# A two-layer encoder on one core: the copy that ends each DMA transpose is queued twelve products behind its issue instead of eight, with three tiles for each of its buffers

## The chip, the cores and the metric

The kernel runs on one NeuronCore of a Trainium2 chip. The metric is the device time of one execution in microseconds (us). The core's engines run side by side, each through its own list of instructions in order: TensorE (PE) multiplies, VectorE (DVE) and ScalarE (ACT) work elementwise, GpSimd (POOL) does some small work, SyncE (SP) issues the DMAs. An instruction that waits holds up everything behind it on its own engine.

## The reference

The input is x with 256 tokens of 1024 float32 values. Two layers follow, then a last RMSNorm:

```python
for layer in range(2):
    h = rms_norm(x, ffn1_norm[layer])
    x = x + 0.5 * swiglu(h, ffn1_w_gate[layer], ffn1_w_up[layer], ffn1_w_down[layer])
    h = rms_norm(x, mix_norm[layer])
    x = x + (even_mixer(h, ...) if layer % 2 == 0 else odd_mixer(h, ...))
    h = rms_norm(x, ffn2_norm[layer])
    x = x + 0.5 * swiglu(h, ffn2_w_gate[layer], ffn2_w_up[layer], ffn2_w_down[layer])
return rms_norm(x, final_norm)

def swiglu(h, w_gate, w_up, w_down):
    return (silu(h @ w_gate) * (h @ w_up)) @ w_down    # 1024 -> 2816 -> 1024
```

The mixers are attention layers; the change does not touch them.

## The kernel before

**Stages.** There are six stages: feed-forward (0), even mixer (1), feed-forward (2), feed-forward (3), odd mixer (4), feed-forward (5). The tokens are two tiles of 128 (tt = 0 and 1). In the trace, stage 0 is about 0 to 205 us, stage 2 about 300 to 525, stage 3 about 525 to 700, stage 5 about 830 to the end.

**Products.** Every float32 weight piece is split into a high part (`hi`, ACT, line 474) and the rest (`lo`, DVE, line 477). A *product* is one call of `mm`: three matmuls (lines 466, 467, 468) of hi x high, lo x high, hi x low, each 128x128 by 128x512. The weights arrive in tiles `raw` through SP's queue (line 376); a `raw` tile is loaded anew once the last `lo` has been made of it.

**A feed-forward stage.** The 2816 hidden values are five chunks of 512 (numbered 0 to 4) and one of 256. In a plain chunk, 16 products make the gates of both token tiles and 16 the ups; for the 256 both lie in one weight piece and 16 products do. One or two chunks of each stage (chunk 2 in stages 0 and 5, chunks 1 and 3 in stages 2 and 3) are done by Strassen's scheme, seven products for eight (`seven_gates`). For those DVE also adds up weight blocks (`two<-raw`, `raw<-two,raw`, line 392) and ACT and DVE split the sums (`shi`, `slo`). Then the *down* part multiplies the gated values by w_down, also partly by sevens, which need sums of gated blocks (`quarters`, `k10h` and the like).

**The turn-over.** The gated values of one chunk and one token tile (`glu`, 128x512) have to be transposed before the down part can use them. [...] After it ACT makes the high part `g_h` (and parts of `quarters`), DVE the rest `g_l`. There are 48 turn-overs: 6 chunks x 2 token tiles x 4 stages.

**What sets the order.** The order of instructions on each engine is that of the Python code; nothing reorders it. Work beside the products is written as generators. `mm` calls `tick` after each product, and each `yield n` means "go on n ticks, that is n products, later". So `TURN_WAIT = [2, 8]` says: issue the DMA 2 products after the first copy, and queue the second copy 8 products after that. The delay is a place in the program, not a time: ACT gets to that place when all ACT work ahead of it is done, and there waits for the DMA. Weight splits are queued by a rate per tick. Tiles `glu` and `turned` come from rings (`bufs`) of 2.

Of the kernel before, what the change touches and what calls it, by code (L numbers as in the profile page):

```python
# [18 lines left out]
P = 128  # L19
# [33 lines left out]
X_WAIT = 5  # L53
R_WAIT = 3
GLU_WAIT = 6
TURN_WAIT = [2, 8]
NAT_WAIT = 2
ROPE_WAIT = [3, 3]
KB_WAIT = {
# [143 lines left out]
class Trunk:  # L203
# [342 lines left out]

    def turned_over(self, m, w):

        two = self.t([P, 512], "turned", 2)
        planes, back = (t.bitcast(U16)[:, : 2 * w] for t in (two, m))  # L550
        self.nc.scalar.copy(planes.rearrange("p (h c) -> p h c", h=2), back.rearrange("p (c h) -> p h c", h=2))  # L551
        yield TURN_WAIT[0]
        self.nc.sync.dma_start_transpose(back.rearrange("p (j t) -> p j t", t=P), planes)
        yield TURN_WAIT[1]
        self.nc.scalar.copy(planes.rearrange("p (c h) -> p h c", h=2), back.rearrange("p (h c) -> p h c", h=2))  # L555
        yield 1
        return two
# [96 lines left out]
    def ffn(self):  # L654
# [13 lines left out]

        def glu(tt, f0, w, u, s):
            yield 1  # L670
            m = self.t([P, 512], "glu", 2)
            nc.vector.scalar_tensor_tensor(m[:, :w], u[:, :w], self.now.r[tt], s[:, :w], op0=ALU.mult, op1=ALU.mult)  # L672
            self.spawn(transposed(tt, f0, w, m), GLU_WAIT)

        def transposed(tt, f0, w, m):
            n = w // P
            tb = yield from self.turned_over(m, w)
            pairs = [f for f in range(f0, f0 + n) if f in paired and f + 1 < f0 + n]
            parts = []
            for f in pairs:  # L680
                yield from quarters(tt, f, tb, f - f0)

            if tt == 1 and f0 + n - 2 in pairs:
                n -= 1
            yield from self.split_psum(tb, n, f"g{tt}_{f0}_", parts)
            for j, part in enumerate(parts):
                gT[tt][f0 + j] = part
            for f in pairs if tt == 1 else []:
                yield from sums_of(f)
# [61 lines left out]
        def seven_gates(f0, w, pairs7):  # L751

            while len(K) < 4:
                self.tick(False)
            self.rate = SEVEN_RATE[self.now.n]
            h, M, c = self.now.hT, {}, {}
            op = nc.vector.tensor_tensor

            def copy():
                yield 1  # L760
                c["m"] = self.t([P, 512], "glu", 2)
                nc.scalar.activation(c["m"], M["1"], AF.Copy)

            def common():

                yield 1
                while "m" not in c:
                    yield 1
                w = self.t([P, 512], "silu", 2)
                op(w, M["6"], c["m"], op=ALU.add)  # L770
                yield 1
                y = self.t([P, 512], "glu", 2)
                op(y, M["5"], w, op=ALU.subtract)
                yield 1
                nc.vector.scalar_tensor_tensor(w, M["7"], -1.0, w, op0=ALU.mult, op1=ALU.add)
                c["y"], c["w"] = y, w

            def first_gate():
                yield 1
                while "m" not in c:  # L780
                    yield 1
                s = self.t([P, 512], "silu", 2)
                op(s, M["00"], c["m"], op=ALU.add)
                yield 1
                nc.scalar.activation(s, s, AF.Silu, scale=self.now.r[0])
                c["s"] = s

            def up(tt, o, u, s):
                nc.vector.scalar_tensor_tensor(o, u, self.now.r[tt], s, op0=ALU.mult, op1=ALU.mult)
                self.spawn(transposed(tt, f0, w, o), GLU_WAIT)  # L790
                yield 1

            def rest():
                yield 1
                while "s" not in c or "w" not in c:
                    yield 1
                y, z, m = c["y"], c["w"], c["m"]
                op(y, M["01"], y, op=ALU.add)
                yield 1
                tasks.append(self.start(up(0, y, y, c["s"])))  # L800
                yield 1
                op(m, M["10"], z, op=ALU.add)
                yield 1
                nc.scalar.activation(m, m, AF.Silu, scale=self.now.r[1])
                op(z, M["5"], z, op=ALU.subtract)
                yield 1
                if "11" in M:
                    op(z, M["11"], z, op=ALU.add)
                    yield 1
                tasks.append(self.start(up(1, m, z, m)))  # L810

            def product(name, lh, piece, first, last):
                self.mm(M[name], lh, piece, first, last)

            n7 = KD // 2 - pairs7
            M.update((name, self.bank(tag)) for name, tag in [("00", "s"), ("01", "s"), ("10", "s")])
            if n7:
                M["11"] = self.bank("o")
            for q in range(KD // 2):
                k, first, last = 2 * q, q == n7, q == KD // 2 - 1  # L820
                if q < n7:
                    pieces = self.take(4)
                    for i in range(2):
                        for n, piece in enumerate(pieces[2 * i : 2 * i + 2]):
                            for tt in range(NT):
                                product(f"{tt}{n}", h[tt][k + i], piece, k + i == 0, tt == n == 1 and i == 1 and q + 1 == n7)
                    continue
                b11, b21, b22, t7, t5, t8, t6 = self.take(7)
                if first:
                    for task in tasks:  # L830
                        self.finish(task)
                    M.update((name, self.bank(tag)) for name, tag in [("1", "pj"), ("5", "pj"), ("7", "tp")])
                    M["6"] = self.bank("tp" if n7 else "o")
                j = q - (KD // 2 - most)
                product("1", h[0][k + 1], b11, first, last)
                if last:
                    self.start(copy())
                product("00", h[0][k], b21, q == 0, last)
                if last:
                    tasks.append(self.start(first_gate()))  # L840
                product("01", K[0][j], b22, q == 0, last)
                product("7", K[3][j], t7, first, last)
                product("5", K[2][j], t5, first, last)
                product("10", h[1][k], t8, q == 0, last)
                product("6", K[1][j], t6, first, last)
            self.start(common())
            tasks.append(self.start(rest()))

# [24 lines left out]
        w, V = FF_MIXED, self.take(KD)  # L873
# [52 lines left out]
        def combine():  # L926

            op = nc.vector.scalar_tensor_tensor
            x = lambda tt, i: self.x[tt][:, i * 512 : i * 512 + 512]
            more = lambda o, y: nc.vector.tensor_tensor(o, o, y, op=ALU.add)  # L930
            yield 1
            c = self.t([P, 512], "silu", 2)
            nc.scalar.activation(c, M["1"], AF.Copy, scale=0.5)
            op(x(0, 0), M["1"], 0.5, x(0, 0), op0=ALU.mult, op1=ALU.add)
            yield 1
            v = self.t([P, 512], "silu", 2)
            op(v, M["6"], 0.5, c, op0=ALU.mult, op1=ALU.add)
            yield 1
            w = self.t([P, 512], "glu", 2)
            op(w, M["7"], -0.5, v, op0=ALU.mult, op1=ALU.add)  # L940
            yield 1
            y = self.t([P, 512], "silu", 2)
            op(y, M["5"], 0.5, v, op0=ALU.mult, op1=ALU.subtract)
            yield 1
            more(x(0, 1), y)
            z = self.t([P, 512], "glu", 2)
            yield 1
            op(z, M["5"], 0.5, w, op0=ALU.mult, op1=ALU.subtract)
            yield 1
            more(x(1, 0), w)  # L950
            yield 1
            more(x(1, 1), z)
# [436 lines left out]
    def after(self, tt, sl, nxt):  # L1389
# [10 lines left out]
        h, w = sl.start // 512, sl.stop - sl.start  # L1400
        half = slice(512 * h, 512 * h + 512)
        x, gain = self.x[tt], self.last_gain
        sq = self.t([P, 512], "sq")
        v = self.two.tile([P, 1], F32, tag="last_v", name=self.name("v"), bufs=6)
        if (tt, h) in ((0, 1), (1, 0)):
            nc.scalar.activation(sq, x[:, sl], AF.Square, scale=D ** -0.5, accum_out=v)
# [8 lines left out]
        elif not h:  # L1415
            a, b = self.last_v[0]
# [146 lines left out]
```

## Time and profile before

| | before |
|---|---|
| median of 3 runs | 1030.58 us (1029.57 to 1031.09) |
| profiled execution, its own time | 1029.36 us |
| span of its trace (first to last instruction) | 1027.6 us |
| mean granted TensorE clock over the span | 0.966 |
| PE busy | 959.0 us (93%), 4399 matmuls |
| DVE busy | 792.7 us (77%) |
| ACT busy | 679.3 us (66%) |
| DMA transposes | 48, landing 5.6 us (median) after the issue, 3.0 to 7.4 |

"Busy" for PE counts matmuls that overlap and also those that run at a lower clock, so 93% is not 93% of what PE could do. A wait is put down to the instruction or DMA that released it. In rows of the timeline, the figure in square brackets at the end is the idle time of the engine just before the instruction, and what ended it.

### The profile page before, as it was taken

The page shows a single profiled execution, that of the slowest core. Times are in us where ns is not written, and L with a number is a line of the kernel's source. Part 1 is how long each engine was busy: PE and PEld are TensorE (multiplying, and loading weights), DVE is VectorE, ACT ScalarE, POOL GpSimd, SP SyncE. Part 2 cuts the span into 40 slices and gives each one's busy share as a digit, 9 for nine tenths or more (in the row PEclk, how much of TensorE's full clock was granted, in tenths as well). Part 3 has the DMA queues.
Part 4 walks back from the last instruction along what each step waited for, and adds up shares of the span by engine and source line. Part 5 has one row for each costly group of instructions (what it writes and reads, how often), then busy time and mean ns, then how long its engine had stood idle before and what let it go on. Part 6 is the DMA issues. An engine that isn't in the chain of part 4 may idle for free.

```text
span 1027.6 us, 12420 instructions
## 1 busy us (share of the span) xinstructions
PE 959.0 (93%) x4399; PEld 769.4 (75%) x4399; DVE 792.7 (77%) x1228; ACT 679.3 (66%) x1091; POOL 87.5 (9%) x152
## 2 busy tenths in 40 slices
PE   9989799999998998889999787899999999988997
PEld 6867588877787776678888576687778888776876
DVE  6787569788878977578977783889777788865698
ACT  7665666468786665575676665666677587656653
POOL 1100000064310000000100000003320000000001
PEclk9999999999999998899999988999999999997999
DMA  8747566554245665666558466375544357566652
GB/s 297 246 141 229 148 225 209 205 148 99 83 128 180 205 199 169 186 191 234 169 161 258 129 196 181 123 265 161 155 150 136 124 168 221 167 202 184 188 194 79
DMA packets 129343, 183.16 MB, mean 178 GB/s; under 512 B 50688, under 2 KB 63744, under 8 KB 129280
## 3 DMA queue, kind: packets, MB, share of 16 engines
q1 hardware_dynamic: 128704, 181.58, 56.6%
q8 instruction: 34, 0.56, 0.2%
q10 hardware_dynamic: 576, 0.79, 0.2%
q14 instruction: 29, 0.24, 0.1%
HBM read 169.76 MB, written 1.05 MB: 166 GB/s over the span
## 4 chain that ended last, share of the span: by engine, by line
PE 44%; DVE 21%; DMA 14%; ACT 14%; issue 5%; SPq 1%; POOL 0%; ACTq 0%; POOLq 0%; DVEq 0%
DMA glu<-turned 11%; DVE lo L477 10%; PE pj L466 7%; PE pj L467 7%; PE pj L468 7%; ACT hi L474 5%; PE s L467 5%; PE s L468 5%; PE s L466 5%; ACT turned L555 3%; DVE slo L477 2%; DVE raw L392 2%; DVE two L392 2%; PE o L1035 2%; ACT turned L551 1%
## 5 line engine op out<-in xcount | busy, mean ns | idle before, releaser
L477 DVE TENSOR_TENSOR lo<-raw,hi 128x1024 fp32r<-128x1024 f32 (+1 forms) x372 | 377.7, 1036 | 96.8 <-ACT hi L474 95.8
L474 ACT ACTIVATE hi<-raw 128x1024 fp32r<-128x1024 f32 (+1 forms) x372 | 316.3, 888 | 42.1 <-DMA raw<-in_ffn_w_gate 8.0
L467 PE MATMUL s<-lo,th 128*128 128x512 f32 x373 | 150.8, 404 | 12.6 <-DVE lo L477 12.6
L466 PE MATMUL s<-hi,th 128*128 128x512 f32 x373 | 150.2, 403 | 9.7 <-ACT hi L474 6.8
L466 PE MATMUL pj<-hi,th 128*128 128x512 f32 x367 | 150.3, 409 | 7.3 <-ACT hi L474 6.8
L467 PE MATMUL pj<-lo,th 128*128 128x512 f32 x367 | 147.2, 401 | 1.9 <-DVE lo L477 1.7
L468 PE MATMUL s<-hi,tl 128*128 128x512 f32 x373 | 148.6, 398 | 0.0
L468 PE MATMUL pj<-hi,tl 128*128 128x512 f32 x367 | 146.2, 398 | 0.0
L555 ACT COPY turned<-glu 128x1024 uint16<-128x1024 uint16 (+1 forms) x48 | 60.0, 1250 | 75.8 <-DMA glu<-turned 75.8
L467 PEld LDWEIGHTS s<-lo,th 128*128 128x128 f32 x373 | 72.1, 193 | 33.2 <-DVE lo L477 18.9
L466 PEld LDWEIGHTS s<-hi,th 128*128 128x128 f32 x373 | 72.1, 193 | 27.8 <-ACT hi L474 9.2
L466 PEld LDWEIGHTS pj<-hi,th 128*128 128x128 f32 x367 | 71.2, 194 | 23.5 <-ACT hi L474 7.6
L467 PEld LDWEIGHTS pj<-lo,th 128*128 128x128 f32 x367 | 71.1, 194 | 18.8 <-DVE lo L477 5.3
L468 PEld LDWEIGHTS s<-hi,tl 128*128 128x128 f32 x373 | 72.2, 194 | 14.7
L468 PEld LDWEIGHTS pj<-hi,tl 128*128 128x128 f32 x367 | 70.8, 193 | 15.0
L486 POOL TENSOR_TENSOR rstd<-var,mhalf 128x1 f32<-128x1 f32 (+2 forms) x16 | 17.1, 1070 | 668.5 <-ACT th L507 361.9
L477 DVE TENSOR_TENSOR g_l<-turned,g_h 128x512 fp32r<-128x512 f32 (+2 forms) x48 | 29.5, 614 | 38.4 <-ACT g_h L474 38.4
L466 PE MATMUL s<-hi,g_h 128*128 128x512 f32 (+1 forms) x131 | 52.7, 402 | 6.1 <-DVE glu L672 6.1
L551 ACT COPY turned<-glu 128x1024 uint16<-128x1024 uint16 (+1 forms) x48 | 46.3, 964 | 15.4 <-DVE glu L672 13.1
L474 ACT ACTIVATE shi<-two 128x1024 fp32r<-128x1024 f32 x30 | 31.8, 1058 | 34.8 <-DVE two L392 34.4
L468 PE MATMUL s<-hi,g_l 128*128 128x512 f32 (+1 forms) x131 | 52.2, 398 | 0.0
L467 PE MATMUL s<-lo,g_h 128*128 128x512 f32 (+1 forms) x131 | 52.1, 397 | 0.0
(483 smaller groups left out, 1694.9 us busy)
## 6 DMA issues: line engine op xcount, KB each, us to landing
raw<-in_ffn_w_down SPq DMA_DIRECT2D x44, 1024.0 KB, 5.2
raw<-in_ffn_w_up SPq DMA_DIRECT2D x28, 1024.0 KB, 5.3
raw<-in_ffn_w_gate SPq DMA_DIRECT2D x26, 1024.0 KB, 5.2
raw<-in_ffn_w_gate SPq DMA_DIRECT2D x35, 512.0 KB, 4.0
raw<-in_ffn_w_up SPq DMA_DIRECT2D x32, 512.0 KB, 5.1
raw<-in_odd_w_qkv SPq DMA_DIRECT2D x12, 1024.0 KB, 5.4
raw<-in_even_w_in SPq DMA_DIRECT2D x4, 1024.0 KB, 5.2
raw<-in_even_w_out SPq DMA_DIRECT2D x8, 512.0 KB, 6.2
```

The lines of the kernel that those rows point to most:

```text
L392: add = lambda o, x, y: self.nc.vector.tensor_tensor(o, x, y, op=ALU.add)
L466: mm(ps, h, wh, start=first, stop=False)
L467: mm(ps, h, wl, start=False, stop=False)
L468: mm(ps, l, wh, start=False, stop=last)
L474: self.nc.scalar.activation(hi, src, AF.Copy)
L477: self.nc.vector.tensor_tensor(lo, src, hi.bitcast(F32), op=ALU.subtract)
L486: nc.gpsimd.tensor_tensor(r[:, :n], v[:, :n], self.mhalf[:, :n], op=ALU.pow)
L551: self.nc.scalar.copy(planes.rearrange("p (h c) -> p h c", h=2), back.rearrange("p (c h) -> p h c", h=2))
L555: self.nc.scalar.copy(planes.rearrange("p (c h) -> p h c", h=2), back.rearrange("p (h c) -> p h c", h=2))
L1035: self.nc.tensor.matmul(O[64 * s : 64 * s + 64, i * P : i * P + P], v(b0 + i, s, kc), pT[s][:, i, kc, :], start=(kc == 0), stop=(kc == 1),)
```

## The change

The second copy is queued 12 products behind the DMA's issue instead of 8. Since a gated tile then lives longer, `glu` and `turned` get rings of 3. That takes 4 KB more per partition in every feed-forward stage; in the last one, the scratch tile `sq` for the final norm's squares is dropped and the tile `quarters`, idle by then, is used in its place.

```diff
-TURN_WAIT = [2, 8]
+TURN_WAIT = [2, 12]
...
     def turned_over(self, m, w):
-        two = self.t([P, 512], "turned", 2)
+        two = self.t([P, 512], "turned", 3)
...
             def glu(tt, f0, w, u, s):
-            m = self.t([P, 512], "glu", 2)
+            m = self.t([P, 512], "glu", 3)
...
     def after(self, tt, sl, nxt):
-        sq = self.t([P, 512], "sq")
+        sq = self.t([P, 4, P], "quarters").rearrange("p a b -> p (a b)")
```

The four other places that take a `glu` tile get the 3 too (in `seven_gates` and `combine`). The number of instructions is the same on every engine, and SP's order does not change. What changes is where the second copies and the work behind them stand.

**Chunk 3 to chunk 4 of stage 0, ACT** (100 to 136 us in the trace). `turned_997` and `turned_1031` are the two token tiles of chunk 3 (993 and 1031 in the changed kernel); `hi` are weight splits for the coming products, `silu_1036` the gate of chunk 4. Before:

```order
L551 COPY turned_997<-glu_948 128x1024
L474 ACTIVATE hi_1012<-raw_911 128x1024
L551 COPY turned_1031<-glu_1007 128x1024
L555 COPY turned_997<-glu_948 128x2x512
L667 ACTIVATE silu_1036<-s_1002,rstd_213 128x512
L696 ACTIVATE quarters_1047<-turned_997 128x256
L474 ACTIVATE g_12_h_1049<-turned_997 128x512
L474 ACTIVATE hi_1052<-raw_911 128x1024
L474 ACTIVATE hi_1065<-raw_964 128x1024
L474 ACTIVATE hi_1075<-raw_964 128x1024
L555 COPY turned_1031<-glu_1007 128x2x512
```

And now, ACT at the same place:

```order
L551 COPY turned_993<-glu_945 128x1024
L474 ACTIVATE k10h_998<-quarters_940 128x512
L474 ACTIVATE hi_1012<-raw_911 128x1024
L551 COPY turned_1031<-glu_1007 128x1024
L667 ACTIVATE silu_1036<-s_1001,rstd_213 128x512
L474 ACTIVATE hi_1046<-raw_911 128x1024
L474 ACTIVATE hi_1058<-raw_958 128x1024
L555 COPY turned_993<-glu_945 128x2x512
L696 ACTIVATE quarters_1069<-turned_993 128x256
L474 ACTIVATE g_12_h_1071<-turned_993 128x512
L474 ACTIVATE hi_1074<-raw_958 128x1024
L667 ACTIVATE silu_1087<-s_1037,rstd_258 128x512
```

The gate and two weight splits now stand ahead of the first second copy, and one split and the next gate between it and the other token tile's.

**Chunk 2 to chunk 3 of stage 2, ACT** (372 to 402 us), where chunk 3 is done by sevens. Before:

```order
L474 ACTIVATE shi_3630<-two_3614 128x1024
L555 COPY turned_3573<-glu_3534 128x2x512
L696 ACTIVATE quarters_3645<-turned_3573 128x256
L474 ACTIVATE g_8_h_3647<-turned_3573 128x512
L555 COPY turned_3628<-glu_3586 128x2x512
L699 ACTIVATE quarters_3645<-turned_3628 128x128
L474 ACTIVATE g_8_h_3685<-turned_3628 128x384
L474 ACTIVATE k10h_3697<-quarters_3645 128x512
L474 ACTIVATE shi_3700<-raw_3483 128x1024
L474 ACTIVATE hi_3710<-raw_3547 128x1024
L474 ACTIVATE hi_3717<-raw_3547 128x1024
L762 ACTIVATE glu_3729<-pj_3669 128x512
```

And now, ACT at the same place:

```order
L474 ACTIVATE shi_3630<-two_3614 128x1024
L555 COPY turned_3573<-glu_3529 128x2x512
L696 ACTIVATE quarters_3657<-turned_3573 128x256
L474 ACTIVATE g_8_h_3659<-turned_3573 128x512
L555 COPY turned_3628<-glu_3586 128x2x512
L474 ACTIVATE shi_3689<-raw_3483 128x1024
L699 ACTIVATE quarters_3657<-turned_3628 128x128
L474 ACTIVATE hi_3699<-raw_3542 128x1024
L474 ACTIVATE g_8_h_3707<-turned_3628 128x384
L474 ACTIVATE hi_3710<-raw_3542 128x1024
L474 ACTIVATE k10h_3725<-quarters_3657 128x512
L762 ACTIVATE glu_3728<-pj_3669 128x512
```

Here both second copies stand where they stood; the splits `shi_3689` and `hi_3699` now come straight behind the second one, ahead of the parts made from it, and `k10h` has moved right in front of the copy on line 762.

**Chunk 1 to chunk 2 of stage 2, DVE** (346 to 372 us): `glu_3534` (3529 now) is the gated product of chunk 2's first token tile. Before:

```order
L477 TENSOR_TENSOR lo_3500<-raw_3409,hi_3499 128x1024
L477 TENSOR_TENSOR g_4_l_3514<-turned_3448,g_4_h_3513 128x512
L672 SCALAR_TENSOR_TENSOR glu_3534<-s_3491,rstd_2940,silu_3439 128x512
L477 TENSOR_TENSOR g_4_l_3532<-turned_3474,g_4_h_3531 128x512
L477 TENSOR_TENSOR lo_3541<-raw_3409,hi_3540 128x1024
```

And now, DVE at the same place:

```order
L477 TENSOR_TENSOR lo_3500<-raw_3409,hi_3499 128x1024
L672 SCALAR_TENSOR_TENSOR glu_3529<-s_3491,rstd_2940,silu_3439 128x512
L477 TENSOR_TENSOR g_4_l_3527<-turned_3448,g_4_h_3526 128x512
L477 TENSOR_TENSOR lo_3536<-raw_3409,hi_3535 128x1024
L477 TENSOR_TENSOR lo_3549<-raw_3457,hi_3548 128x512
```

The gated product, which frees a PSUM bank, now stands ahead of the low part of the turned-over tile instead of behind it.

More of the change, by code (lines that the diff above doesn't have):

```diff
@@ L760, in copy @@
                 yield 1
-                c["m"] = self.t([P, 512], "glu", 2)
+                c["m"] = self.t([P, 512], "glu", 3)
                 nc.scalar.activation(c["m"], M["1"], AF.Copy)
@@ L771, in common @@
                 yield 1
-                y = self.t([P, 512], "glu", 2)
+                y = self.t([P, 512], "glu", 3)
                 op(y, M["5"], w, op=ALU.subtract)
@@ L938, in combine @@
             yield 1
-            w = self.t([P, 512], "glu", 2)
+            w = self.t([P, 512], "glu", 3)
             op(w, M["7"], -0.5, v, op0=ALU.mult, op1=ALU.add)
@@ L945, in combine @@
             more(x(0, 1), y)
-            z = self.t([P, 512], "glu", 2)
+            z = self.t([P, 512], "glu", 3)
             yield 1
```

## The prediction, made before the run

> **What bounds the kernel now.** I read the page first, then the waits, then the timeline around the longest of them, then a table by stretches. The page's engine line, its chain that ended last, and the group of the second copies:
>
> ```profile
> PE 959.0 (93%) x4399; PEld 769.4 (75%) x4399; DVE 792.7 (77%) x1228; ACT 679.3 (66%) x1091; POOL 87.5 (9%) x152
> DMA glu<-turned 11%; DVE lo L477 10%; PE pj L466 7%; PE pj L467 7%; PE pj L468 7%; ACT hi L474 5%; PE s L467 5%; PE s L468 5%; PE s L466 5%; ACT turned L555 3%; DVE slo L477 2%; DVE raw L392 2%; DVE two L392 2%; PE o L1035 2%; ACT turned L551 1%
> L555 ACT COPY turned<-glu 128x1024 uint16<-128x1024 uint16 (+1 forms) x48 | 60.0, 1250 | 75.8 <-DMA glu<-turned 75.8
> ```
>
> PE is the busiest, but the longest item of the chain is not PE: it is the DMA transpose, and ACT stands 75.8 us before second copies. The waits by total show who stands behind ACT:
>
> ```profile
> DVE lo L477 <- ACT hi L474: 95.8, 81, 8.3
> ACT turned L555 <- DMA glu<-turned: 75.8, 31, 4.9
> DVE g_l L477 <- ACT g_h L474: 38.4, 12, 5.0
> ACT turned L551 <- DVE g_l L477: 2.2, 3, 1.2
> ```
>
> Columns: total us, times, longest. 31 of the 48 second copies wait, and DVE waits for ACT's high parts. The timeline of stage 0, ACT and then PE (start, us, instruction, idle before):
>
> ```profile
> 115.67 1.05 ACT L551 COPY turned<-glu 128x1024 uint16<-128x1024 uint16 x1 [0.90 <-DVE glu L672]
> 121.38 1.33 ACT L555 COPY turned<-glu 128x1024 uint16<-128x1024 uint16 x1 [4.67 <-DMA glu<-turned]
> 122.58 0.67 ACT L667 ACTIVATE silu<-s,rstd 128x512 f32<-128x512 f32 x1
> 123.98 2.94 ACT L474 ACTIVATE hi<-raw 128x1024 fp32r<-128x1024 f32 x3
> ```
>
> ```profile
> 119.65 0.39 PE L467 MATMUL pj<-lo,th 128*128 128x512 f32 x1
> 119.88 0.39 PE L468 MATMUL pj<-hi,tl 128*128 128x512 f32 x1
> 125.07 0.80 PE L466 MATMUL pj<-hi,th 128*128 128x512 f32 x1 [4.80 <-ACT hi L474]
> 127.35 0.63 PE L466 MATMUL pj<-hi,th 128*128 128x512 f32 x1
> 127.78 0.63 PE L467 MATMUL pj<-lo,th 128*128 128x512 f32 x1
> ```
>
> ACT waits 4.67 us for a DMA while the weight splits that PE needs next are queued behind the copy; PE runs dry for 4.80 us. And it is paid twice: matmuls start 0.23 us apart before the gap and 0.43 us apart after it. The granted clock is halved for a while.
>
> The third view adds both losses up by stretches (us, then busy time of PE, PEld, DVE, ACT, POOL with counts, then the granted clock):
>
> ```profile
> 60.00:100.00 40.00, 36.28 (x145) 27.48 (x144) 32.40 (x38) 25.02 (x31) 0.00 (x0) 0.96 0.61 192
> 100.00:136.00 36.00, 28.65 (x109) 21.70 (x108) 19.39 (x26) 24.15 (x31) 0.00 (x0) 0.91 0.59 176
> 300.00:346.00 46.00, 42.80 (x180) 34.16 (x179) 40.51 (x55) 32.72 (x43) 1.49 (x1) 0.96 0.54 172
> 346.00:372.00 26.00, 24.47 (x107) 19.60 (x106) 17.93 (x21) 16.22 (x20) 0.00 (x0) 1.00 0.69 222
> 372.00:402.00 30.00, 24.75 (x95) 19.28 (x94) 24.14 (x30) 20.35 (x25) 0.00 (x0) 0.89 0.54 161
> 402.00:446.00 44.00, 37.92 (x144) 29.61 (x144) 25.25 (x31) 26.27 (x33) 0.00 (x0) 0.88 0.59 172
> 545.00:572.00 27.00, 25.66 (x113) 20.90 (x112) 17.73 (x22) 15.10 (x19) 0.00 (x0) 1.00 0.65 200
> 572.00:602.00 30.00, 22.20 (x83) 16.54 (x82) 23.68 (x31) 21.31 (x26) 0.00 (x0) 0.89 0.55 165
> 602.00:645.00 43.00, 37.34 (x150) 29.81 (x149) 24.55 (x32) 24.46 (x31) 0.00 (x0) 0.92 0.59 177
> 645.00:665.00 20.00, 17.10 (x67) 13.19 (x67) 17.24 (x24) 13.62 (x20) 0.00 (x0) 0.91 0.37 118
> 850.00:902.00 52.00, 50.16 (x217) 39.89 (x216) 42.92 (x54) 36.67 (x46) 0.00 (x0) 1.00 0.67 190
> 902.00:950.00 48.00, 42.61 (x160) 33.67 (x159) 29.18 (x38) 31.26 (x39) 0.00 (x0) 0.86 0.62 190
> ```
>
> PE's loss in a stretch is its idle time plus (1 - clock) x length. For 402 to 446 us: 44.00 - 37.92 = 6.1, and 0.12 x 44 = 5.3, together 11.4. In the same way: 5.3, 10.6, 5.0, 1.5, 8.6, 11.4, 1.3, 11.1, 9.1, 4.7, 1.8, 12.1 us, in the order of the rows. The sum, 82.5 us, is the most that could be had.
>
> **The change, part by part.** Nothing is added or removed; second copies and what hangs on them stand four products later, 4 x 3 x 0.23 = 2.7 us of PE time.
>
> *A: after a chunk by sevens or a plain chunk, with plain products next (100 to 136, 402 to 446, 602 to 645, 902 to 950; at stake 10.6 + 11.4 + 9.1 + 12.1 = 43.2).* In stage 0 the gate and two splits now run right after the first copy that ends at 116.7: 0.67 for the gate, then 2.94 / 3 = 1.0 each for the splits, done at 119.4. PE wants them at 120.1. So the 4.80 us gap goes, and the half clock that follows it (0.09 x 36 = 3.2). Each of the other three has such a place too. Before it, each stretch has one more, where the first second copy keeps its neighbours (in stage 0 one split passes it) and goes on waiting, but a split comes in front of the other token tile's copy. I take four fifths, 34.6: a fifth stays where ACT still has to wait with little ahead of PE. Ends: 12 (half of the idle time, 24.5 / 2, and the clock as it is) and 43.
>
> *B1: the second chunk by sevens in stages 2 and 3 (372 to 402, 572 to 602; 8.6 + 11.1).* ACT and PE there:
>
> ```profile
> 386.55 1.33 ACT L555 COPY turned<-glu 128x1024 uint16<-128x1024 uint16 x1 [1.56 <-DMA glu<-turned]
> 389.85 0.63 ACT L474 ACTIVATE k10h<-quarters 128x512 fp32r<-128x512 f32 x1 [1.21 <-DVE quarters L710]
> 390.39 1.04 ACT L474 ACTIVATE shi<-raw 128x1024 fp32r<-128x1024 f32 x1
> 391.48 0.80 PE L466 MATMUL s<-shi,th 128*128 128x512 f32 x1 [4.34 <-ACT shi L474]
> ```
>
> The copy still waits for the DMA, since nothing moves ahead of it, but the split `shi` follows it at 387.9 instead of 390.4. That is 2.5 us of a gap of 4.34; some 2 us stay. Is that enough to halve the clock? A gap of that size elsewhere:
>
> ```profile
> 425.03 0.72 PE L466 MATMUL s<-hi,th 128*128 128x512 f32 x1 [1.96 <-ACT hi L474]
> 425.10:431.90 6.80, 6.26 (x14) 4.64 (x15) 5.06 (x8) 4.42 (x5) 0.00 (x0) 0.50 0.49 157
> ```
>
> A 1.96 us gap opens 6.8 us at clock 0.50, so I leave the 3.3 us of each place as lost: 2 x 2.5 = 5.0. [...]
>
> *B2: the rest.* In 346 to 372 and its twin 545 to 572, DVE stood before `g_l` with the gated product behind it:
>
> ```profile
> 366.96 0.69 DVE L477 TENSOR_TENSOR g_l<-turned,g_h 128x512 fp32r<-128x512 f32 x1 [4.04 <-ACT g_h L474]
> 367.57 0.75 DVE L672 SCALAR_TENSOR_TENSOR glu<-s,rstd,silu 128x512 f32<-128x512 f32 x1
> ```
>
> Now the gated product stands ahead, and 1.5 + 1.3 = 2.8 us go. In the other four (5.3 + 5.0 + 4.7 + 1.8 = 16.8) DVE is busy 32.40 of 40, 40.51 of 46, 17.24 of 20 and 42.92 of 52 us with block sums and low parts, which stay. I take a quarter, 4.2; ends 0 and 12.
>
> *What costs nothing.* The parts come four products later, but in the program the closest first use (hidden block 20 of stage 3) was 13 products behind its part and is 9 behind now, 6.1 us, covered by other down products; the next are 13 and 15. SP issues in the same order; its transposes wait for the first copies only, which keep their places or come earlier. The rings' third tile is needed for the longer life; by itself it could remove the 2.2 us above, on ACT. The shared scratch tile is idle when it is taken over.
>
> *What comes instead.* PE takes weights faster. Splits already wait for loads:
>
> ```profile
> L474 ACT ACTIVATE hi<-raw 128x1024 fp32r<-128x1024 f32 (+1 forms) x372 | 316.3, 888 | 42.1 <-DMA raw<-in_ffn_w_gate 8.0 <-DMA raw<-in_ffn_w_up 7.7 <-PE s L468 6.7
> ```
>
> Of 8.0 + 7.7 = 15.7 us nothing much reaches PE now. I put 6 us on PE for the faster pace, nearer the low end of 0 to 16, as the DMA share in the stretches above is 0.7 at most.
>
> *Sum:* 34.6 + 5.0 + 2.8 + 4.2 - 6 = 40.6 us. The profiled execution took 1029.4 us (span 1027.6), 1.2 under the median, so 1029.4 - 40.6 = 988.8, and against the median of 1030.6: **990 us**.
>
> **Rivals.**
>
> 1. *The wait only moves.* The DMA lands when it lands; ACT stops a little later, with PE's stock used up, and the clock still falls. For it: three of the four A stretches keep the first copy's neighbours. Against it: at 119.4 the splits are there before PE asks. Then A gives 12, B little: about 1030.6 - 15 = 1016 us. Chance 0.17.
>
> 2. *Nearly all goes.* A and B1 in full and the twins of B2, 43.2 + 19.7 + 2.8 = 65.7: 965 us. For it: the gaps feed each other, since each delays the loads and splits of the next. Against it: the copies in B1 still wait. Chance 0.12.
>
> 3. *Slower: the chunks by sevens pay.* `k10h` now stands right in front of line 762, the copy that frees a PSUM bank for PE. These rows are its price:
>
> ```profile
> 110.33 0.63 ACT L474 ACTIVATE k10h<-quarters 128x512 fp32r<-128x512 f32 x1 [2.35 <-DVE quarters L710]
> 894.18 0.50 PE L466 MATMUL pj<-hi,th 128*128 128x512 f32 x1 [0.54 <-ACT glu L762]
> ```
>
> If ACT waits 2.35 + 0.63 = 3.0 us there with PE behind it in all six such chunks, and each halves the clock (3.4), that is 6 x 6.4 = 38 us. It decides if A, B1 and B2 give under 38; with a gain of 15, 1054 us. PE has waited for line 762 only 0.54 us. Chance 0.05.
>
> 4. *It doesn't do what it says*, PE being held elsewhere all the time: 1030 us, 0.03.
>
> **How the numbers follow.** The forecast has 0.63. The 8-in-10 range runs from 965 (rival 2) to 1015 (just under rival 1), which leaves out half of each and rivals 3 and 4. A difference under 0.2% can't be told from none here. Faster 0.92, same 0.03, slower 0.05.
>
> **What would show it.** Right: ACT's idle time before line 555 falls from 75.8 us to under 45; PE's gaps behind `hi` in A under 1 us; the granted clock there over 0.96; in B1 `shi` straight behind the second copy with some 2 us of gap. Wrong: as many half-clock spells as before; PE waiting for `glu` of line 762; splits waiting for `raw` far over 16 us with PE behind them; or first uses of `g_h` and `g_l` among PE's waits.

## The result, and the profile after

The changed kernel takes 984.6 us (median of 4 runs, 983.8 to 987.1) against 1030.1 us of the kernel before (median of 4): a ratio of 0.9565, 95% interval 0.9542 to 0.9587. The trace spans 982.8 us, 44.8 less than before. The prediction said 990, range 965 to 1015.

The page of the changed kernel, the same three rows as shown of the kernel before:

```profile
PE 935.0 (95%) x4399; PEld 755.6 (77%) x4399; DVE 792.7 (81%) x1228; ACT 677.2 (69%) x1091; POOL 94.4 (10%) x152
DVE lo L477 9%; PE pj L466 7%; DMA glu<-turned 7%; PE pj L468 7%; PE pj L467 7%; PE s L467 6%; PE s L468 6%; PE s L466 6%; ACT hi L474 5%; DVE raw L392 2%; DVE two L392 2%; DVE slo L477 2%; ACT shi L474 2%; PE o L1035 2%; PE tp L1114 1%
L555 ACT COPY turned<-glu 128x1024 uint16<-128x1024 uint16 (+1 forms) x48 | 60.1, 1251 | 40.7 <-DMA glu<-turned 40.5
```

In a turn-over, line 551 is the first copy (it takes the float32 values apart into planes of upper and lower halves), line 553 the DMA transpose, line 555 the second copy (it puts the halves together again): 48 of each in both traces, the copies on uint16 elements (128x1024 in 40, 128x512 in 8). DVE and ACT are busy for as long as before (792.7 us, and 677.2 against 679.3), within a shorter span. The transpose's share of the chain falls from 11% to 7%, and ACT's idle time before second copies from 75.8 to 40.7 us. The waits (total us, times, longest):

```profile
DVE lo L477 <- ACT hi L474: 85.9, 94, 4.0
ACT turned L555 <- DMA glu<-turned: 40.5, 22, 3.5
DVE g_l L477 <- ACT g_h L474: 23.5, 7, 4.3
PE pj L466 <- ACT glu L762: 5.7, 2, 3.4
```

The last row was 0.5 us before. The stage 0 place of the prediction, on ACT:

```profile
109.46 1.05 ACT L551 COPY turned<-glu 128x1024 uint16<-128x1024 uint16 x1 [0.47 <-DVE glu L672]
110.42 0.69 ACT L667 ACTIVATE silu<-s,rstd 128x512 f32<-128x512 f32 x1
111.00 2.00 ACT L474 ACTIVATE hi<-raw 128x1024 fp32r<-128x1024 f32 x2
112.90 1.35 ACT L555 COPY turned<-glu 128x1024 uint16<-128x1024 uint16 x1
```

The gate and two splits run where ACT used to stand for 4.67 us, and the copy then waits for nothing. The table by stretches, each cut at the same product as its row of before (found by counting products). The columns are those of the prediction's table; the last three figures are the granted clock, the share of time that the DMA engines are busy, and GB/s:

```profile
60.00:96.50 36.50, 33.93 (x145) 26.54 (x144) 30.51 (x37) 24.54 (x30) 0.00 (x0) 1.00 0.58 181
96.50:121.00 24.50, 24.50 (x109) 20.04 (x108) 15.36 (x22) 19.75 (x26) 0.00 (x0) 1.00 0.85 244
284.80:331.30 46.50, 41.29 (x181) 33.01 (x179) 40.56 (x55) 32.77 (x43) 1.49 (x1) 1.00 0.54 170
331.30:355.60 24.30, 24.30 (x108) 19.81 (x107) 17.94 (x20) 14.70 (x17) 0.00 (x0) 1.00 0.78 238
355.60:387.50 31.90, 25.68 (x94) 19.61 (x93) 24.20 (x30) 22.13 (x28) 0.00 (x0) 0.84 0.51 152
387.50:423.40 35.90, 33.30 (x145) 26.63 (x144) 23.91 (x29) 22.71 (x29) 0.00 (x0) 1.00 0.71 205
522.30:547.50 25.20, 25.20 (x112) 20.81 (x111) 17.34 (x21) 15.74 (x20) 0.00 (x0) 1.00 0.75 224
547.50:578.00 30.50, 21.70 (x83) 16.23 (x82) 23.81 (x32) 20.27 (x26) 0.00 (x0) 0.94 0.54 169
578.00:612.90 34.90, 34.34 (x150) 27.58 (x149) 25.78 (x32) 22.82 (x29) 0.00 (x0) 1.00 0.71 212
612.90:631.90 19.00, 16.83 (x67) 13.49 (x66) 17.69 (x25) 16.67 (x24) 0.00 (x0) 0.91 0.46 140
812.40:865.50 53.10, 49.90 (x217) 40.14 (x216) 43.19 (x54) 37.73 (x47) 0.00 (x0) 1.00 0.64 188
865.50:903.40 37.90, 36.35 (x159) 29.57 (x158) 25.29 (x31) 26.99 (x34) 0.00 (x0) 1.00 0.72 213
```

The lengths against those of before: the four A stretches are 11.5, 8.1, 8.1 and 10.1 us shorter (second, sixth, ninth and last row), PE idles 4.7 us in the four together, 24.5 before, and the clock stays at 1.00. The twins of B2 gain 1.7 and 1.8. The two B1 stretches (fifth and eighth row) are 1.9 and 0.5 us *longer*. Their rows on ACT, then PE:

```profile
370.94 1.33 ACT L555 COPY turned<-glu 128x1024 uint16<-128x1024 uint16 x1 [1.57 <-DMA glu<-turned]
372.15 1.04 ACT L474 ACTIVATE shi<-raw 128x1024 fp32r<-128x1024 f32 x1
378.16 0.63 ACT L474 ACTIVATE k10h<-quarters 128x512 fp32r<-128x512 f32 x1 [2.46 <-DVE quarters L710]
378.69 0.58 ACT L762 ACTIVATE glu<-pj 128x512 f32<-128x512 f32 x1
```

```profile
373.24 0.50 PE L466 MATMUL s<-shi,th 128*128 128x512 f32 x1 [1.72 <-ACT shi L474]
379.32 0.80 PE L466 MATMUL pj<-hi,th 128*128 128x512 f32 x1 [2.32 <-ACT glu L762]
```

The split stands straight behind the second copy and PE's gap there shrank from 4.34 to 1.72 us; but then ACT waits 2.46 us for DVE's block sums before `k10h`, line 762 is behind that, and PE waits 2.32 us for its bank.

### The profile page after: what moved, and what is told of

Read it like the earlier page. It is cut to its first block, busy times and chain, and to the rows that moved or that the text cites. A ratio compares the mean times of both kernels' runs of the same rounds, so it can differ in the third digit from the quotient of the medians.

```text
span 982.8 us, 12398 instructions
## 1 busy us (share of the span) xinstructions
PE 935.0 (95%) x4399; PEld 755.6 (77%) x4399; DVE 792.7 (81%) x1228; ACT 677.2 (69%) x1091; POOL 94.4 (10%) x152
## 4 chain that ended last, share of the span: by engine, by line
PE 50%; DVE 21%; ACT 13%; DMA 9%; issue 6%; SPq 1%; POOL 1%; POOLq 0%; ACTq 0%; DVEq 0%
DVE lo L477 9%; PE pj L466 7%; DMA glu<-turned 7%; PE pj L468 7%; PE pj L467 7%; PE s L467 6%; PE s L468 6%; PE s L466 6%; ACT hi L474 5%; DVE raw L392 2%; DVE two L392 2%; DVE slo L477 2%; ACT shi L474 2%; PE o L1035 2%; PE tp L1114 1%
## 5 line engine op out<-in xcount | busy, mean ns | idle before, releaser
L467 PE MATMUL s<-lo,th 128*128 128x512 f32 x373 | 147.0, 394 | 10.9 <-DVE lo L477 10.9
L466 PE MATMUL s<-hi,th 128*128 128x512 f32 x373 | 146.3, 392 | 0.4 <-ACT hi L474 0.4
L468 PE MATMUL s<-hi,tl 128*128 128x512 f32 x373 | 145.5, 390 | 0.0
L467 PEld LDWEIGHTS s<-lo,th 128*128 128x128 f32 x373 | 70.0, 188 | 30.5 <-DVE lo L477 16.6
L466 PEld LDWEIGHTS pj<-hi,th 128*128 128x128 f32 x367 | 70.1, 191 | 24.5 <-ACT glu L762 6.9
L555 ACT COPY turned<-glu 128x1024 uint16<-128x1024 uint16 (+1 forms) x48 | 60.1, 1251 | 40.7 <-DMA glu<-turned 40.5
L466 PEld LDWEIGHTS s<-hi,th 128*128 128x128 f32 x373 | 70.0, 188 | 14.8 <-ACT hi L474 0.6
L468 PEld LDWEIGHTS s<-hi,tl 128*128 128x128 f32 x373 | 70.1, 188 | 14.1
L477 DVE TENSOR_TENSOR slo<-raw,shi 128x1024 fp32r<-128x1024 f32 x30 | 36.7, 1222 | 21.1 <-ACT shi L474 21.1
```

The source lines that it names most:

```text
L466: mm(ps, h, wh, start=first, stop=False)
L467: mm(ps, h, wl, start=False, stop=False)
L468: mm(ps, l, wh, start=False, stop=last)
L477: self.nc.vector.tensor_tensor(lo, src, hi.bitcast(F32), op=ALU.subtract)
```

## The experiments

Ratios are to the kernel before, from runs on the same chip; its median there was 1028 to 1029 us. The theory: ACT stands at the head of its queue for a DMA, and PE pays for the splits and gates behind it.

**The two halves of the change.** Delay 12 with rings of 2, and rings of 3 with delay 8:

```diff
# first kernel, against before         # second kernel, against after
-TURN_WAIT = [2, 8]                    -TURN_WAIT = [2, 12]
+TURN_WAIT = [2, 12]                   +TURN_WAIT = [2, 8]
```

> Delay 12 with the rings of `glu` and `turned` left at 2. Theory (the place of the second copies is what counts; the third tiles only give the longer life room): most of the gain stays, 985 to 1002 us, with new waits of DVE's gated product or of the first copies for a tile where three gated tiles follow each other quickly (chunk 4 and the chunk of 256, 2 waits of about 2 us in each of four stages). Rival (the third tiles are the gain): 1015 us or more.

Measured: 1006.6 us, ratio 0.9772 (0.9755 to 0.9789). About half of the gain; the time is longer than the 985 to 1002 us that were expected. The waits of this kernel:

```profile
DVE glu L672 <- ACT turned L555: 52.1, 13, 7.1
ACT turned L555 <- DMA glu<-turned: 37.8, 21, 3.5
ACT turned L551 <- DVE g_l L477: 27.1, 8, 5.7
```

ACT's wait for the DMA fell as far as in the changed kernel, but the gated product now waits for a tile (the first row, none of it before), and the first copy for another (2.2 us before). I had the mechanism and priced it at 16 us; it is 52 plus 27 us of waiting on two engines.

> Rings of 3 with the delay left at 8. Theory: the only waits for a tile in the profile before were 2.2 us on ACT, so 1028 to 1031 us, and ACT's idle time before the second copies stays at 70 to 80 us. Rival (third tiles are the gain): 985 to 1005 us.

Measured: 1028.5 us, ratio 0.9999 (0.9984 to 1.0013): nothing, as the theory said (ACT's idle time before second copies is 80.9 us, where 70 to 80 were expected). The third tiles gain nothing by themselves and are worth 22 us (1006.6 - 984.6) once tiles live longer.

**Is half of the loss the clock?** The kernel before, with PE's idle time filled by matmuls that nothing reads:

```diff
+FILL = {147: 19, 499: 8, 512: 13, 756: 8, 769: 12, 1109: 8, 1125: 8}   # number of the product: matmuls
     def mm(...):
+        if self.count in FILL:
+            t = self.hts[self.now.n, 0][0]
+            spare = self.bank("tp")
+            for _ in range(FILL[self.count]):
+                self.nc.tensor.matmul(spare, t[:, 0, :], t[:, 0:4, :].rearrange("p a b -> p (a b)"), start=True, stop=True)
```

> The kernel before, with idle PE time filled: ahead of the seven products before which PE stood longest in the four A stretches (4.80, 1.96, 3.19, 2.02, 2.88, 1.88, 1.99 us) stand 19, 8, 13, 8, 12, 8 and 8 matmuls that no one reads, a little shorter than the gap. No wait goes; only the clock should stay up. Theory (half of the gain is the clock, 0.09 x 36 + 0.12 x 44 + 0.08 x 43 + 0.14 x 48 = 18.7 us in A): 1012 to 1020 us, clock of the span 0.98 or more. Rival (while the clock is halved ACT and DVE set the pace anyway): 1027 to 1033 us although the clock is up.

Measured: 1033.1 us, ratio 1.0032 (1.0018 to 1.0047). The four A stretches of this kernel, cut at the same products:

```profile
101.10:137.60 36.50, 31.46 (x125) 24.18 (x124) 18.70 (x25) 23.48 (x30) 0.00 (x0) 0.95 0.61 170
403.50:445.40 41.90, 37.84 (x164) 30.19 (x163) 22.93 (x30) 24.16 (x30) 0.00 (x0) 1.00 0.57 167
603.20:646.70 43.50, 39.41 (x171) 31.75 (x170) 24.34 (x31) 24.79 (x31) 0.00 (x0) 1.00 0.60 171
901.70:949.80 48.10, 43.30 (x174) 34.46 (x173) 27.43 (x37) 29.44 (x37) 0.00 (x0) 0.93 0.65 184
```

The clock is 0.95, 1.00, 1.00, 0.93 where it was 0.91, 0.88, 0.92, 0.86. By the formula of the prediction that is worth (0.04 x 36 + 0.12 x 44 + 0.08 x 43 + 0.07 x 48) = 13.5 us. The four stretches together are 170.0 us long where they were 171. The rival's time is what was measured: the fill brings nothing. Its reason, that at the full clock PE only comes sooner to the next split that ACT has not made, shows at one of the filled products of 902 to 950 (in this kernel line 470 is the fill, and the later lines stand 7 further down):

```profile
920.07 1.98 PE L470 MATMUL tp<-th 128*128 128x512 f32 x8
923.62 0.50 PE L473 MATMUL s<-hi,th 128*128 128x512 f32 x1 [1.58 <-ACT hi L481]
```

PE is through with the fill and still waits 1.58 us for the split; in the kernel before, the same product started at 923.02, no later. One thing blurs the test. In the profiled execution the transposes landed later than before, 5.9 us after the issue (median) and 9.5 at most, against 5.6 and 7.4, and ACT's idle time before second copies rose from 75.8 to 87.3 us. Two waits of 950 to 990, where no matmul was added, on ACT (3.67 and 2.07 us before):

```profile
963.06 1.33 ACT L562 COPY turned<-glu 128x1024 uint16<-128x1024 uint16 x1 [7.03 <-DMA glu<-turned]
983.68 0.77 ACT L562 COPY turned<-glu 128x512 uint16<-128x512 uint16 x1 [3.23 <-DMA glu<-turned]
```

Together they are 4.5 us longer, most of the 5 us or so by which that stretch is longer. Why these DMAs landed later is not shown, nor how much of the clock's 13.5 us they used up in the four stretches. The shortest of the ten runs, 1029.5 us, is still no shorter than the median of before.

**How much is the wait at all?** Both kernels without the transposes. The second copy then reads the planes' source in its untransposed order:

```diff
-        self.nc.sync.dma_start_transpose(back.rearrange("p (j t) -> p j t", t=P), planes)
-        ...copy(planes..., back.rearrange("p (h c) -> p h c", h=2))
+        ...copy(planes..., back.rearrange("p (c h) -> p h c", h=2))
```

> The kernel before without the 48 DMA transposes (the gated values stay unturned); all rows of ACT, DVE and PE keep their places, rings 2 and delay 8. Theory (ACT's wait for the DMA at the head of its queue costs PE): at or under the changed kernel, 965 to 985 us. Rival (the gain comes from the later place of the parts made from the turned tile, not from the wait): above 1010 us.

> The changed kernel (delay 12, rings 3) without the 48 DMA transposes; the gated values stay unturned. The kernel before without them took 960.8 us. Theory (the change works only by the wait; the later place and the third tiles are worth nothing of their own): 957 to 965 us. Rivals: the later place of the parts costs something that the shorter wait hides, 966 us or more; or it gains something by itself, 955 us or less.

Measured: 960.8 us, 0.9339 (0.932 to 0.9359), and 956.8 us, 0.9298 (0.9284 to 0.9311). With every row at its old place and only the DMA gone, 68 us go: it is the wait. (The transposes also leave the queue to the weights, but that is not what PE gets: ACT waits 21.8 us for the feed-forward weights without them and 21.9 with them.) With the wait gone, the later place changes 0.4%; just under the theory's lower end, it may gain a little of its own, and it costs nothing. The changed kernel has got 45 of these 68 us. In A it has nearly all: without transposes at delay 8 these stretches are 42 us shorter than before, in the changed kernel 38. In B1 it has none: there 9 us go without transposes, and the changed kernel is 2 us longer.

**The chunks ahead of the sevens.** The delay back at 8 there, or on to 16:

```diff
-            tb = yield from self.turned_over(m, w)
+            tb = yield from self.turned_over(m, w, 8 if <the next chunk is done by sevens> else None)   # or 16
```

> The changed kernel with the delay back at 8 for the turn-overs of the chunk just ahead of a chunk by sevens (six chunks), 12 elsewhere. Against the kernel before, the changed one gained 3.5 us in 60 to 100, and lost 0.5, 1.9, 0.5 and 1.1 us in 300 to 346, 372 to 402, 572 to 602 and 850 to 902. Theory (these places neither gained nor lost by the delay, all gain is in front of plain products): 983 to 987 us, with PE's wait for line 762 back from 5.7 to under 1 us. Rival (the wait for line 762 is a real price of the change): 976 to 981 us.

Measured: 982.9 us, 0.9545 (0.9528 to 0.9563). Within the interval of the changed kernel (0.9542 to 0.9587): the delay of 12 gains nothing in front of the sevens. PE's wait for line 762 is back at 1.4 us (under 1 was expected), but in return PE waits 8.8 us for `shi` in two places, as before the change.

> The same with 16 there instead of 8. Theory: at 12 nothing passes the second copies in front of the chunks by sevens, at 16 another split or two do, and `k10h` falls behind line 762: 974 to 981 us, PE's wait for line 762 under 2 us. Rival (DVE's block sums hold these chunks whatever ACT does): 983 to 988 us.

Measured: 973.4 us, 0.9456 (0.9442 to 0.947), a little better than expected. PE waits 1.8 us for line 762, ACT 30.0 us for transposes. The B1 stretches are 4.8 and 7.2 us shorter than before the change, instead of longer.

**The wait behind the wait.** `k10h` and its like three products later, so that DVE has the sums ready:

```diff
             nc.vector.tensor_tensor(k[:, 0, :], k[:, 1, :], k[:, 0, :], op=ALU.add)
-            yield 1
+            yield 4
             hi, lo = (self.t([P, 4, P], f"k{f}{p}", 1, F32R) for p in "hl")
```

> The changed kernel with the high part of the block sums (`k10h` and the like) three products later, so that DVE has the sums ready and line 762 is not behind that wait. ACT waits 21.5 us for the sums in the changed kernel, and PE 5.7 us for line 762. Theory (line 762 behind `k10h` is what the two later chunks by sevens pay): 976 to 981 us, and PE waits under 2 us for line 762. Rival (it is the second copy ahead of both that makes line 762 late): 983 to 988 us.

Measured: 970.1 us, 0.943 (0.941 to 0.945), better than expected. The waits of this kernel:

```profile
ACT turned L555 <- DMA glu<-turned: 41.1, 24, 3.6
ACT k6h L474 <- DVE quarters L710: 2.4, 1, 2.4
PE pj L466 <- ACT glu L762: 0.3, 1, 0.3
```

The second copies wait as long as in the changed kernel, and PE's 5.7 us before line 762 are gone; so it was `k10h`, not the second copy, that made line 762 late. ACT's waits for all seven such sums together fall from 28.9 to 8.2 us (the 21.5 us of the expectation are four of the seven). About 10 of the 14 us gained lie in the two B1 stretches.

> The kernel before (delay 8, rings 2) with only the block sums' high parts three products later. Theory (ACT's wait for DVE's sums is a second wait at the head of its queue, behind the second copy; at delay 8 the copy holds PE anyway): 1018 to 1027 us. Rival (the wait for the sums costs the same 14 us by itself): 1012 to 1017 us.

Measured, the same edit in the kernel before: 1011.2 us, 0.9836 (0.9817 to 0.9855). The theory of this run falls: the wait for the sums costs 17 us by itself, at delay 8 too. ACT's waits for the sums fall from 32.4 to 10.7 us here, those for transposes stay (76.6 us). ACT's wait for DVE is a second loss of the same kind, and I had taken it for one that only appears when the first has gone.

**How long must the delay be?** Rings of 3 in all, delay 10 and 16 for all, and 16 ahead of the sevens with the later sums:

```diff
-TURN_WAIT = [2, 12]
+TURN_WAIT = [2, 10]   # the next kernel: [2, 16]; the last: 12, 16 ahead of the sevens, and yield 4
```

> Rings of 3, delay 10 for all. Theory (the delay counts by the splits and gates that pass the second copy; at 10 the gate and one split pass in front of the second turn-over of each A stretch, not two): about half of the gain, 1000 to 1012 us. Rival (a threshold at the landing, 5.5 us or 8 products after the issue, beyond which any delay does): 984 to 992 us.

> Rings of 3, delay 16 for all. Theory: the waits of about 3.4 us that stay at the first copies of five chunks cost PE little now, the chunks by sevens gain as with 16 there alone (11 us), and the gated values of the chunk of 256 wait a little for the ring, as the tiles live 26 products and the ring comes round after 24: 970 to 980 us. Rival (the ring of 3 is too short at 16, as 2 was at 12): 985 us or more.

> The changed kernel with both: 16 for the turn-overs just ahead of a chunk by sevens, and the block sums' high parts three products later. Alone they gave 973.4 and 970.1 us against 984.6. Theory (one frees the splits behind the second copy, the other ACT's wait for DVE's sums; partly the same gap in 372 to 402 and 572 to 602): 963 to 968 us. Rival (both close the same gap): 969 to 972 us.

Measured: 1012.6 us (0.9848, 0.9833 to 0.9863) at 10, 962.2 us (0.9357, 0.9343 to 0.9371) at 16, and 960.7 us (0.934, 0.9324 to 0.9356) for the last; these two can't be told apart, and they are the fastest of the kernels that have the transposes. Both are faster than expected. ACT's waits before second copies in the kernels with delay 10 and 16:

```profile
ACT turned L555 <- DMA glu<-turned: 58.4, 27, 4.1
```

```profile
ACT turned L555 <- DMA glu<-turned: 10.5, 6, 2.7
```

So 8, 10, 12 and 16 products with rings of 3 give 1028.5, 1012.6, 984.6 and 962.2 us, with 81, 58, 41 and 10 us of waiting: 12 is not the end. At 10 the time lies just past the slow end of what was expected, but the reason given there, that fewer splits pass the copies in A, does not account for it. At 10 the A stretches are already 32 us shorter than before (38 at 12), so for A alone the rival, a threshold near the landing, is not ruled out. What is missing at 10 lies elsewhere: 950 to 990 is 7 us longer than before, and there ACT waits 5.9 us, not 2.5, for the sums of `k16h`:

```profile
ACT k16h L474 <- DVE quarters L710: 10.3, 3, 5.9
```

From 12 to 16 it is B1 that gains: its two stretches get some 10 and 12 us shorter, while A gets about 4 us longer. The ring of 3 was feared too short at 16 and is not.

At 16 the time is close to that of the kernel before without any transposes (962.2 against 960.8 us), so most of that loss is hidden. The last kernel's 960.7 us does not show the same: it still waits 34.0 us for transposes, but only 10.5 us for DVE's sums, for which the kernel without transposes still waits 31.9 us.

## Why the prediction was right, and where its steps were not

- **A** (34.6 us of 43.2): 11.5 + 8.1 + 8.1 + 10.1 = 37.8 us. Place and mechanism were right: the splits pass the copy, and the rows of stage 0 above show them there.
- **The clock's part of A and B1** was wrong as an account. 18.7 us of the 43.2 were put down to the halved clock as a loss beside the idle time. In the filled kernel the clock was kept up and nothing was gained, with the reservation on its later transposes. The sum held in A all the same, because idle and slow time of PE went together when ACT's splits came in time.
- **B1** (5.0 us): -1.9 - 0.5 = -2.4 us. The step "the split follows the copy 2.5 us sooner" came true (PE's gap is 1.72 instead of 4.34 us), and so did the assumption that the gap left would still halve the clock (0.84 in the first of the two). What failed is that nothing else was charged there: the price of rival 3, `k10h` in front of line 762, was paid in these two chunks (2.32 us in the row above and 3.4, the longest of the two waits), not in all six.
- **B2**: the twins 1.7 + 1.8 = 3.5 us (2.8 said); the other four 3.5 - 0.5 - 1.1 + 1.0 = 2.9 us (4.2 said). Together 0.6 us under the 7.0 forecast. That DVE's block sums hold the other four was not tested.
- **What comes instead** (6 us for weight loads): did not come. ACT's longest total wait for a load is 8.0 us as before, that for `up` fell from 7.7 to 3.5, that for `down`, which the term left out, from 6.2 to 3.5, and the stretches outside the table are 3.0 us shorter in sum (44.8 less the 41.8 of the points above).
- **What costs nothing**: right for SP's order and for the third tile by itself (no difference measured).
- The sum, 40.6 us, came out at 44.8. A 3.2, outside 3.0 and the loads 6 us better; B1 7.4 and B2 0.6 us worse. The time is right partly because these cancel, which is luck.
- **Rival 1** (the wait only moves) was not borne out in A. In B1 PE's loss did move, but to DVE's sums and line 762, not to a later landing. **Rival 3**'s sign, PE waiting for line 762, was seen, at 5.7 us and not 38 (its 3.4 us a place for the clock is half of the 6.80 us at clock 0.50 in the row of B1). **Rival 2**'s 965 us is reached, but by a delay of 16, not 12.

## What to carry to other kernels

On an engine that works through its list in order, an instruction that waits for a DMA costs what is queued behind it (here 68 us of 1029, by the kernel without the transposes); place it by what can pass it, count the tiles that then live longer, and check what each move puts next to the following wait. Where an engine is starved, don't price its slow clock as a loss of its own before a run has shown it: here filling the gaps raised the clock of the A stretches (0.86 to 0.92 before, 0.93 to 1.00 filled) and gained nothing (1033.1 us against 1029.0). After such a wait is shortened, read the same engine's next waits in turn: here a second one, 17 us, lay beside the first.

## What was not expected of the hardware

In these traces a longer gap left the clock at 1.00 where shorter ones were followed by half clock. In the changed kernel, PE stood 2.58 us in the stretch 284.8 to 331.3, whose clock is 1.00:

```profile
317.37 0.50 PE L467 MATMUL s<-lo,th 128*128 128x512 f32 x1 [2.58 <-DVE lo L477]
```

In 355.6 to 387.5 gaps of 1.72 and 0.76 us were followed by 10.24 us at half clock (0.84 over the stretch), and in the kernel before the 1.96 us of the prediction's row, with 0.54 us behind it, by 6.83 us.

All but the last spells at half clock in the traces of before and after are 3.41, 6.83 or 10.24 us long. What sets their length, and which gaps one follows, is not shown.

The transposes landed 5.5 us (median) after their issue with 186 GB/s on the DMA engines, 5.6 us before with 178 GB/s: the median was no longer in the faster kernel. The longest took 8.1 us, 7.4 before.
